# Last copies of the values in one tile of the input weights' buffers, attention's buffers allocated around it, and the expert gathers issued in order

## The chip, the cores and the metric

The kernel runs on one NeuronCore of one Trainium2 chip. The metric is the device time of one execution in microseconds (us). The kernel before was run three times; the median is what the change is compared with.

## What is computed

One block of a hybrid encoder in float32, with T = 1024 tokens and a width of 1024 (quoted with the parts that matter here; shapes in the comments are mine):

```python
proj = h @ w_in[l]                      # one projection for both mixers
aq, ak, av, iq, ik, iw, bq, bk, bv, br, bg = jnp.split(proj, split_points, axis=-1)
...                                     # rotary embedding of aq, ak, iq, ik
ya = dsa_mixer(aq, ak, av, iq, ik, iw)  # 8 heads of 64; each token sees the 256 best keys
...                                     # log_a from bg
ob = gla_mixer(bq, bk, bv, log_a)       # 4 heads, chunked linear attention
...
mix = jnp.concatenate([ya, yb], axis=-1) @ w_out[l]
h = layer_norm(DEEPNORM_ALPHA * h + mix, ln1_g[l], ln1_b[l])
ffn = hier_moe(h, ...)                  # router picks 2 of 32 experts per token
h = layer_norm(DEEPNORM_ALPHA * h + ffn, ln2_g[l], ln2_b[l])
```

An expert is `silu(x @ Wg) * (x @ Wu)` followed by a second product; its results are scaled by the gate and summed per token.

## The kernel before, in words

Float32 products are made as three products of split operands: each operand is cast to a high part (`whi`, `ehi`, `m`, `xh` ...) on ScalarE and the low part (`wlo`, `elo`, `xl` ...) is the difference, made on VectorE or GpSimd. The stages follow one another:

- **Input projections, index scores, top-k and the linear attention**, in an order chosen by a scheduler. The last product is `values(1, ...)` (L680): the attention values of the second half of the heads, four tiles of results in PSUM, each copied by ScalarE to a tile `vs` and stored by GpSimd's queue to the buffer `d_av` in HBM (L687, L688). The input weights live in a pool `wpool` whose raw, high and low weights have tags (`wraw`, `whi`, ...) with two or three buffers each.
- **Attention** (`attention`, L820 on), in an order written out by hand (`manual_schedule`): 32 items, four head pairs `hp` by eight query tiles `t`. For each item PE makes scores (`s`, L839), VectorE adds the selection bias and takes the maximum (`Sm`, `mx`, L844), ScalarE takes the exponential (L852), PE turns the weights (`pt`, L863), ScalarE or VectorE copies them out of PSUM to a tile `PT` (L866, L868), and PE multiplies them with the values into `ot` (L877). After every fourth query tile GpSimd spreads the reciprocals of the sums into `rb` (L910), PE turns them (L885), and the result goes to a tile `R` (L887, L888) and to the buffer `d_mix`. Attention's pool is allocated over the memory that `wpool` and the rest of the first stage give up, so its first writes into a place wait for the last readers of what lay there.
- **Output product, LayerNorm and router** (`out_phase`, L1007 to L1159), eight token tiles. For each tile the normalized row `r` is stored to `d_h` (which the experts gather from); then `r` is multiplied by ALPHA and stored to `d_y` (to which the experts' results are added). For tiles 0 to 6 that is `rows_out`; for tile 7 it is written out at the end (L1151, L1155, L1156). Meanwhile three pieces of the first expert's weights are split (`split_early`).
- **The change to the experts**: the route of the last tile gives `tok`, the list of tokens of each expert (`tok`, L1263). GpSimd gathers the rows of expert 0 and of expert 1 from `d_h` into `xg0` and `xg1` with indirect DMAs (L1427); `xg1` is set to zero first (L1319). Between them GpSimd makes `rvg` (L1267), from which the gates of the last tile come.
- **The expert stream** (`expert_stream`): 32 experts, each with four pieces of first-layer weights and two of second-layer weights, streamed by SyncE's queue. `ahead()` splits the next piece; `rows_in` issues the gather and turns the rows (L1420). A loop for experts with over 128 tokens and the last LayerNorm follow.

DMA queues keep the order of their engine: SP (SyncE) carries the weights and most loads, ACT carries the stores of `rows_out`, POOL (GpSimd) the gathers and the stores of the values.

Of the kernel before, what the change touches and what calls it, by code (L numbers as in the profile page):

```python
# [9 lines left out]
F32 = mybir.dt.float32  # L10
# [4 lines left out]
U32 = mybir.dt.uint32  # L15
AF = mybir.ActivationFunctionType
OP = mybir.AluOpType
# [3 lines left out]
T = 1024  # L21
# [143 lines left out]
class Kern:  # L165
# [514 lines left out]
    def values(self, g, w, tiles, queue=None):  # L680
        nc = self.nc
        queue = queue or nc.sync
        for t in tiles:

            vs = self.wpool.tile([128, 2, 2, 128], F32, name="vs", tag="wraw" if g and t > 2 else "vs", bufs=3 if g and t > 2 else 2)
            ps = yield from self.proj_n_steps(w, t)
            nc.scalar.copy(vs, ps.rearrange("p t (a b) -> p a t b", a=2))  # L687
            queue.dma_start(self.d_av[g][:, :, t:t + 2, :].rearrange("a p t c -> p a t c"), vs)  # L688
# [131 lines left out]
    def attention(self, p, before):  # L820
# [60 lines left out]
        def shares(s):  # L881

            rp = self.bank("pt", [128, 4, 128])
            for i in range(4):
                nc.tensor.transpose(rp[:, i, :], s["rb"][:, 2 * i:2 * i + 2, :].rearrange("p a b -> p (a b)"), ident)  # L885
            R = p.tile([128, 4, 128], F32, name="R", bufs=2)
            nc.scalar.copy(R.rearrange("p a b -> p (a b)"), rp.rearrange("p a b -> p (a b)"))  # L887
            nc.vector.tensor_mul(R, R, s["ot"])  # L888
            nc.sync.dma_start(self.d_mix[s["t"] // 4][:, :, s["hp"], :].rearrange("t p q -> p t q"), R)

        rec = ot = done = None
        with self.tc.manual_schedule(engines={mybir.EngineType.PE, mybir.EngineType.Activation, mybir.EngineType.DVE}):
            for n in range(len(items) + 2):
                new, turn = n if n < len(items) else None, n - 1 if 0 < n <= len(items) else None
                if new is not None:
                    hp, t = items[n]
                    loads = before(n)
                    if t % 4 == 0:
                        rec = p.tile([128, 4, 2], F32, name="rec", bufs=2)
                    st[n] = {"hp": hp, "t": t, "W": 128 * (t + 1), "S": [], "PT": [], "rec": rec, "loads": loads}  # L900
                if turn is not None:
                    s = st[turn]
                    if s["t"] % 4 == 0:
                        ot = self.bank("ot", [128, 4, 128])
                    s["ot"] = ot
                    if s["t"] % 4 == 3:
                        rb = s["rb"] = p.tile([128, 8, 64], F32, name="rb", bufs=2)
                        rr = p.tile([128, 8], F32, name="rr", bufs=2)
                        nc.vector.reciprocal(rr, s["rec"].rearrange("p a b -> p (a b)"))
                        nc.gpsimd.tensor_copy(rb, rr.unsqueeze(2).to_broadcast([128, 8, 64]))  # L910
                for hd in range(2):
                    if new is not None:
                        scores(new, hd)
                    if turn is not None:
                        turned(turn, hd)
                    if new is not None:
                        weights(new, hd)
                over, done = done, mixed(n - 2) if n > 1 else None
                if over:
                    shares(over)  # L920
            shares(done)
# [85 lines left out]
    def out_phase(self, ctx, weights):  # L1007
# [10 lines left out]
        with self.pool("outp") as p, self.pool("outm") as pm:  # L1018
# [52 lines left out]
                for j in range(4 * n, 4 * n + 4):  # L1071
                    nc.tensor.matmul(lg[:, :36], rT[:, j, :], wr[:, j, :], start=j == 0, stop=j == 7)  # L1072

            def rows_out(t, h):
                nc.scalar.dma_start(self.d_h[t * 128:(t + 1) * 128], h)

                nc.scalar.activation(h, h, AF.Copy, scale=ALPHA)
                nc.scalar.dma_start(self.d_y[t * 128:(t + 1) * 128], h)

            common = wsum, rb, g8, ones, before, lp  # L1080
            pending = None
            for t in range(NT - 1):
                mh, ml, x = operands(t)
                r = p.tile([128, D], F32, name="r", bufs=2)
                rT = p.tile([128, 8, 128], F32, name="rT")
                m, rs, half = self.moments(p, r)
                for n in range(2):
                    ps = self.bank("acc", [128, 512])
                    product(ps, n, range(8), mh, ml)
                    residual(r, x, ps, n)  # L1090
                    half(n)
                for n in range(2):
                    turned(r, rT, n)
                if t < NT - 2:
                    self.centre(r, m, gain)
                    self.scale(r, rs, shift)
                    with tc.issue_after(self.last_act.ins):
                        rows_out(t, r)

                if pending:  # L1100
                    for _ in self.route(p, *pending, *common):
                        pass
                lg = self.bank("ot", [128, 128])
                if t < NT - 2:
                    for n in range(2):
                        logits(lg, rT, n)
                pending = t, lg, m, rs

            mh, ml, x = operands(t + 1)
            r6, rT6, rs6, m6, lg6 = r, rT, rs, m, lg  # L1110
            r = p.tile([128, D], F32, name="r", bufs=2)
# [5 lines left out]
            with tc.manual_schedule(engines={mybir.EngineType.PE, mybir.EngineType.Activation, mybir.EngineType.DVE}):  # L1117
# [6 lines left out]
                steps = self.route(p, *pending, *common)  # L1124
                next(steps)
                self.scale(r6, rs6, shift)
                rows_out(t, r6)
                residual(r, x, ps[0], 0)
                half(0)
                turned(r, rT, 0)  # L1130
                product(ps[1], 1, range(4, 8), mh, ml)
                for _ in steps:
                    pass
# [14 lines left out]
                steps = self.route(p, t + 1, lg, m, rs, *common)  # L1148
                next(steps)
                self.scale(r, rs, shift)  # L1150
                nc.sync.dma_start(self.d_h[(t + 1) * 128:(t + 2) * 128], r)  # L1151
                for _ in steps:
                    pass
                early[1][0]()
                nc.scalar.activation(r, r, AF.Copy, scale=ALPHA)  # L1155
                nc.scalar.dma_start(self.d_y[(t + 1) * 128:(t + 2) * 128], r)  # L1156
                for e in early:
                    e[1]()
            self.lp = lp  # L1159

    def split_early(self):
# [29 lines left out]
    def route(self, p, t, lg, m, rs, wsum, rb, g8, ones, before, lp):  # L1191
# [69 lines left out]
        if end:  # L1261

            nc.vector.tensor_scalar(self.tok, lp[:, :, 0], float(PAD), None, op0=OP.add)  # L1263
            gates()
            rvg = [keep.tile([128, NE], F32, name=f"rvg{k}") for k in range(2)]
            for k in range(2):
                nc.gpsimd.tensor_scalar(rvg[k], self.oh[:, t, k, :], val[:, k, 1:2], None, op0=OP.mult)  # L1267

            def finish():
                for k in range(2):  # L1270
                    nc.tensor.matmul(lp[:, :, 1], sls[k], rvg[k], start=False, stop=k == 1, skip_group_check=True)
                nc.vector.tensor_copy(self.lists, lp)

            self.finish_gates = finish

    def count_blocks(self):
        nc, ones = self.nc, self.ones
# [18 lines left out]
    def experts(self):  # L1296
# [5 lines left out]
        with self.pool("exp") as self.ep:  # L1302
# [11 lines left out]
            with tc.manual_schedule(engines={mybir.EngineType.PE, mybir.EngineType.Activation, mybir.EngineType.DVE}):  # L1314
                third = self.split_early()
                third[0]()
                x = self.rows_in(self.xg[0], cols(0)[0])
                with tc.issue_after(self.last_gather.ins):
                    nc.gpsimd.memset(self.xg[1], 0.0)  # L1319
                third[1]()  # L1320
                self.expert_stream(cols, x, work)
            self.last_mm = None
# [14 lines left out]
    def expert_stream(self, cols, x, work):  # L1337
# [30 lines left out]
        for e in range(NE):  # L1368
            hg, hu = (self.bank("acc", [128, 512]) for _ in range(2))
            for q in range(4):  # L1370
# [5 lines left out]
                if q == 1:  # L1376
                    if e:

                        ah = self.turn_act(act)
                    else:  # L1380

                        x1 = self.rows_in(self.xg[1], cols(1)[0], ("y", "y"), 2)
                if e == 0 and q == 3:

                    self.ready.append(self.split_piece(self.piece()))
                    self.early.close()
                    self.wp = work.enter_context(self.pool("work"))
                elif q < 3:
                    ahead()
            act = self.gate_up(hg, hu)  # L1390
            if e:
# [29 lines left out]
                                                       src[:, 128 * (b + i):128 * (b + i) + 128], self.c["ident"])  # L1421
            self.split(hi[:, b:b + 4, :].rearrange("p a b -> p (a b)"), lo[:, b:b + 4, :].rearrange("p a b -> p (a b)"), pt)

    def rows_in(self, xg, tok, tags=("xh", "xl"), bufs=1):

        nc, p = self.nc, self.ep
        self.last_gather = nc.gpsimd.indirect_dma_start(out=xg, out_offset=None, in_=self.d_h,  # L1427
                                     in_offset=bass.IndirectOffsetOnAxis(ap=tok.bitcast(U32), axis=0),
                                     bounds_check=T - 1, oob_is_err=False)
        xh, xl = (p.tile([128, 8, 128], F32R, name=n, tag=t, bufs=bufs) for n, t in zip(("xh", "xl"), tags))  # L1430
        self.turn(xg, 8, xh, xl)
        return xh, xl
# [52 lines left out]
    def more_blocks(self):  # L1485
# [11 lines left out]
        we = self.I["we"].rearrange("e k c -> (e k) c")  # L1497
        wf = self.I["wf"].rearrange("e k c -> (e k) c")
        n = nc.values_load(self.nmore[0:1, 0:1], min_val=0, max_val=2 * T // 128)
        self.last_mm = None  # L1500
        with tc.For_i(0, n, 1):
            eh = p.tile([128, NE], F32, name="eh")
            e2 = p.tile([128, NE], F32, name="e2")
# [127 lines left out]
```

## Time and profile before

| what | value |
|---|---|
| median of 3 runs | 1294.08 us (1291.38 to 1295.2) |
| the profiled execution's own time | 1292.31 us |
| its span in the trace | 1290.5 us |
| mean granted TensorE clock | 0.97 |
| PE, DVE, ACT, POOL busy | 93%, 80%, 61%, 31% of the span |
| weights of the experts, 690 to 1200 us | 364 GB/s, PE 510.00 us busy |

The span is the time from the first to the last instruction of the trace; the execution's own time is 1.81 us longer. The rows quoted further down come from this one execution, and their start times are microseconds from the start of the span. A name in square brackets at a row's end says how long the engine had been idle and what released it.

### The profile page before, as it was taken

The numbers are of one execution on the slowest core, as the hardware profiler recorded it, in microseconds if no ns is written. First come the engines' busy times: TensorE is split into PE (matmuls) and PEld (weight loads), VectorE is DVE, ScalarE is ACT, GpSimd is POOL, SyncE is SP. The second block draws the span as 40 slices with busy tenths as digits, with TensorE's granted clock in tenths as the row PEclk, the third lists the DMA queues.
The fourth block names the chain that finished last, engine by engine and source line by source line (L and its number), as shares of the span: only waits on it lengthen the run. The fifth ranks groups of instructions, "written<-read, shape, count | busy, mean of one in ns | idle before, by whom it ended". The sixth has DMA issues, their size and how long they took to land.

```text
span 1290.5 us, 19395 instructions
## 1 busy us (share of the span) xinstructions
PE 1204.2 (93%) x6926; PEld 1003.1 (78%) x6926; DVE 1028.6 (80%) x1657; ACT 792.8 (61%) x1112; POOL 394.5 (31%) x354
## 2 busy tenths in 40 slices
PE   6999999999996999999859999999999999999962
PEld 5979988877795888888747888888888888888851
DVE  4567897999993666477768999889998899889945
ACT  4378366665534667132257777777777777777835
POOL 2532642345753453011121321112221222122215
PEclk9999999999998999999979999999999999999985
DMA  7653544325468661874378999999999999999926
GB/s 257 163 180 99 191 156 126 112 61 143 105 186 242 190 170 58 308 278 164 131 271 313 375 372 367 382 368 360 380 365 369 351 361 357 352 356 353 321 44 260
DMA packets 133588, 322.61 MB, mean 250 GB/s; under 512 B 20953, under 2 KB 50546, under 8 KB 133490
## 3 DMA queue, kind: packets, MB, share of 16 engines
q1 hardware_dynamic: 109826, 280.92, 61.4%
q0 software_dynamic: 15168, 26.27, 8.1%
q10 hardware_dynamic: 8496, 14.16, 3.3%
q8 instruction: 55, 0.90, 0.3%
q14 instruction: 43, 0.35, 0.1%
HBM read 283.78 MB, written 54.26 MB: 262 GB/s over the span
## 4 chain that ended last, share of the span: by engine, by line
PE 73%; DVE 8%; DMA 6%; ACT 5%; another core or an unknown queue 3%; POOL 3%; issue 3%; SPq 0%; ACTq 0%; POOLq 0%; DVEq 0%
PE acc L1353 26%; PE ot L1353 13%; PE acc L1057 7%; PE acc L236 5%; PE acc L222 4%; PE pt L1420 3%; PE ot L877 3%; DVE eq L723 3%; PE s L839 2%; PE pt L863 2%; PE g L236 1%; DMA d_mix<-ym 1%; PE ot L1072 1%; PE g L222 1%
## 5 line engine op out<-in xcount | busy, mean ns | idle before, releaser
L181 DVE TENSOR_TENSOR elo<-big,ehi 128x2048 fp32r<-128x2048 f32 (+1 forms) x132 | 268.0, 2062 | 21.9 <-ACT ehi L180 20.2
L180 ACT CAST ehi<-big 128x2048 fp32r<-128x2048 f32 (+1 forms) x132 | 223.0, 1727 | 0.0
L1353 PE MATMUL acc<-ehi,xh 128*128 128x512 f32 x512 | 206.4, 403 | 2.0 <-ACT sg L1469 2.0
L1353 PE MATMUL acc<-ehi,xl 128*128 128x512 f32 x512 | 203.3, 397 | 0.0
L1353 PE MATMUL acc<-elo,xh 128*128 128x512 f32 x512 | 203.2, 397 | 0.0
L1427 POOL DMA_INDIRECT xg<-d_h,tok x32 | 36.8, 1151 | 360.8 <-PE pt L1420 360.3
L222 PE MATMUL acc<-big,whi 128*128 128x512 f32 (+1 forms) x384 | 120.3, 392 | 10.0 <-ACT big L180 10.0
L1406 POOL DMA_INDIRECT d_y<-y,tok x32 | 96.2, 3006 | 105.8 <-ACT ehi L180 50.2
L236 PE MATMUL acc<-whi,big 128*128 128x256 f32 x672 | 125.4, 286 | 0.0
L1353 PEld LDWEIGHTS acc<-ehi,xh 128*128 128x128 f32 x512 | 96.7, 189 | 24.5 <-ACT sg L1469 2.4
L1353 PEld LDWEIGHTS acc<-ehi,xl 128*128 128x128 f32 x512 | 96.6, 189 | 23.6 <-DVE xl L181 0.3
L1353 PEld LDWEIGHTS acc<-elo,xh 128*128 128x128 f32 x512 | 97.0, 189 | 22.0
L236 PEld LDWEIGHTS acc<-whi,big 128*128 128x128 f32 x672 | 105.6, 192 | 1.8 <-issue 1.0
L723 DVE TENSOR_SCALAR_CACHE_REDUCE eq<-sc,cand 128x384 bf16<-128x384 f32 (+1 forms) x124 | 100.5, 810 | 7.0 <-POOL sc L735 4.6
L1353 PE MATMUL ot<-ehi,ah 128*128 128x512 f32 x256 | 104.1, 407 | 0.4 <-ACT ah L180 0.4
L181 DVE TENSOR_TENSOR elo<-slot,ehi 128x2048 fp32r<-128x2048 f32 (+1 forms) x46 | 95.5, 2102 | 7.8 <-ACT ehi L180 7.3
L1353 PE MATMUL ot<-ehi,al 128*128 128x512 f32 x256 | 101.5, 397 | 0.0
L1353 PE MATMUL ot<-elo,ah 128*128 128x512 f32 x256 | 101.4, 396 | 0.0
L753 ACT ACTIVATE sn<-sc,cand 128x896 bf16<-128x896 f32 (+1 forms) x62 | 68.0, 1097 | 46.5 <-DVE cand L749 36.5
L236 PE MATMUL acc<-wlo,big 128*128 128x256 f32 x336 | 95.8, 285 | 0.0
L222 PEld LDWEIGHTS acc<-big,whi 128*128 128x128 f32 x384 | 72.5, 193 | 25.1 <-ACT big L180 10.0
L1057 PE MATMUL acc<-wohi,m 128*128 128x512 f32 x256 | 86.0, 405 | 0.0
(297 smaller groups left out, 2601.6 us busy)
## 6 DMA issues: line engine op xcount, KB each, us to landing
big<-we SPq DMA_DIRECT2D x79, 1024.0 KB, 15.8
big<-wf SPq DMA_DIRECT2D x40, 1024.0 KB, 20.2
slot<-we SPq DMA_DIRECT2D x26, 1024.0 KB, 14.0
sc<-we SPq DMA_DIRECT2D x20, 1024.0 KB, 20.2
slot<-wf SPq DMA_DIRECT2D x16, 1024.0 KB, 23.2
wraw<-wi SPq DMA_DIRECT2D x52, 256.0 KB, 3.2
sc<-wf SPq DMA_DIRECT2D x8, 1024.0 KB, 10.5
raw<-xT SPq DMA_DIRECT2D x8, 512.0 KB, 6.9
```

The source lines that it names most:

```text
L180: nc.scalar.copy(hi, src)
L181: (lo_eng or nc.vector).tensor_tensor(lo, src, hi.bitcast(F32), op=OP.subtract)
L222: nc.tensor.matmul(ps[:m, :n], l[:, j, c0:c0 + m], r[:, j % 2, t0:t0 + n], start=(j == 0 and a == 0), stop=(j == 7 and a == 2))
L236: nc.tensor.matmul(ps[:, i, :], l[:, j % 2, s], r[:, j, :], start=(j == 0 and a == 0), stop=(j == 7 and a == 2))
L723: nc.vector.tensor_scalar(gtt[:, :WS[i]], x, v, 0.0, op0=op, op1=OP.add, accum_out=cnt[:, i:i + 1])
L753: nc.scalar.activation(jnk[:, :WS[i]], y[i], AF.Sign, bias=c, accum_out=cnt[:, i:i + 1])
L877: nc.tensor.matmul(ot[r, t % 4, :], v[:, b, r], s["PT"][hd][:, b, :], start=b == 0, stop=b == t)
L1057: nc.tensor.matmul(ps, l[:, j, :], w[:, j, s], start=(j == 0 and a == 0), stop=(j == 7 and a == 2))
L1353: nc.tensor.matmul(o, x[:, jj, :], w[:, j, s], start=(jj == 0 and a == 0), stop=(jj == n - 1 and a == 2))
L1406: nc.gpsimd.indirect_dma_start(out=self.d_y, out_offset=bass.IndirectOffsetOnAxis(ap=tok.bitcast(U32), axis=0), in_=y, in_offset=None, bou ...
L1420: self.last_mm = nc.tensor.transpose(pt[:, 128 * i:128 * i + 128], src[:, 128 * (b + i):128 * (b + i) + 128], self.c["ident"])
L1427: self.last_gather = nc.gpsimd.indirect_dma_start(out=xg, out_offset=None, in_=self.d_h, in_offset=bass.IndirectOffsetOnAxis(ap=tok.bitcas ...
```

## The change

The copies of the last product go into slices of one tile `whole` that uses a buffer of the tag `whi`, where the tiles `vs` were. In attention, the two buffers of `rb` and the two of `R` are allocated ahead of all others (with equal shapes), so that these lie over `whole` and the others elsewhere. `rows_out` writes the scaled rows to another tile than `r` (tile 6's to its `x`, tile 7's to `rT`), tile 6's call moves behind a turn, tile 7's ahead of the rest of the route, and the two early low parts are made in the other order. At the change to the experts GpSimd issues the memset and the gathers of expert 0 and 1 before `rvg`, and in the first expert one `ahead()` moves ahead of the turning of expert 1's rows.

```diff
@@ values
+        whole = self.wpool.tile([128, 4, 2, 2, 128], F32, name="whole", tag="whi", bufs=2) if g else None
         for t in tiles:
-
-            vs = self.wpool.tile([128, 2, 2, 128], F32, name="vs", tag="wraw" if g and t > 2 else "vs", bufs=3 if g and t > 2 else 2)
+            vs = whole[:, t // 2] if g else self.wpool.tile([128, 2, 2, 128], F32, name="vs", bufs=2)
@@ attention
+        for name in ("rb", "R"):
+            for _ in range(2):
+                p.tile([128, 512], F32, name=name, bufs=2)
         with self.tc.manual_schedule(engines={mybir.EngineType.PE, mybir.EngineType.Activation, mybir.EngineType.DVE}):
@@ out_phase
-            def rows_out(t, h):
-                nc.scalar.dma_start(self.d_h[t * 128:(t + 1) * 128], h)
-
-                nc.scalar.activation(h, h, AF.Copy, scale=ALPHA)
-                nc.scalar.dma_start(self.d_y[t * 128:(t + 1) * 128], h)
+            def rows_out(t, h, x, queue):
+                queue.dma_start(self.d_h[t * 128:(t + 1) * 128], h)
+
+                nc.scalar.activation(x, h, AF.Copy, scale=ALPHA)
+                nc.scalar.dma_start(self.d_y[t * 128:(t + 1) * 128], x)
...
-                rows_out(t, r6)
                 residual(r, x, ps[0], 0)
                 half(0)
                 turned(r, rT, 0)
+                rows_out(t, r6, x6, nc.scalar)
...
-                nc.sync.dma_start(self.d_h[(t + 1) * 128:(t + 2) * 128], r)
+                rows_out(t + 1, r, rT.rearrange("p a b -> p (a b)"), nc.sync)
                 for _ in steps:
                     pass
                 early[1][0]()
-                nc.scalar.activation(r, r, AF.Copy, scale=ALPHA)
-                nc.scalar.dma_start(self.d_y[(t + 1) * 128:(t + 2) * 128], r)
-                for e in early:
+                for e in reversed(early):
                     e[1]()
+                self.ready.reverse()
@@ experts
-                x = self.rows_in(self.xg[0], cols(0)[0])
+                self.last_gather = nc.gpsimd.memset(self.xg[1], 0.0)
+                for e in range(2):
+                    self.gather(self.xg[e], cols(e)[0])
                 with tc.issue_after(self.last_gather.ins):
-                    nc.gpsimd.memset(self.xg[1], 0.0)
+                    self.start_gates()
+                x = self.turn_rows(self.xg[0])
@@ expert_stream
-                        x1 = self.rows_in(self.xg[1], cols(1)[0], ("y", "y"), 2)
+                        ahead()
+                        x1 = self.turn_rows(self.xg[1], ("y", "y"), 2)
...
-                elif q < 3:
+                elif q < 3 and (e or q != 1):
                     ahead()
```

`start_gates()` makes the two `rvg`; `gather` is the indirect DMA of `rows_in`, `turn_rows` is its rest.

GpSimd at the change to the experts stood like this before (`rvt` and `rvg` are the routed tables of the last tile, `xg_7168` is expert 0's and every second later expert's gathered rows, `xg_7279` expert 1's):

```order
L1227 TENSOR_SCALAR rvt<-oh,K 128x32 x2
L1267 TENSOR_SCALAR rvg_7250<-oh,val 128x32
L1267 TENSOR_SCALAR rvg_7251<-oh,val 128x32
L1427 DMA xg_7168<-d_h,tok 128x1024
L1319 MEMSET xg_7279 128x1024
L1427 DMA xg_7168<-d_h,tok 128x1024
L1427 DMA xg_7279<-d_h,tok 128x1024 x2
```

And it stands like this after (`xg_7169` is expert 0's, `xg_7278` expert 1's):

```order
L1232 TENSOR_SCALAR rvt<-oh,K 128x32 x2
L1324 MEMSET xg_7278 128x1024
L1443 DMA xg_7169<-d_h,tok 128x1024
L1443 DMA xg_7278<-d_h,tok 128x1024
L1274 TENSOR_SCALAR rvg_7253<-oh,val 128x32
L1274 TENSOR_SCALAR rvg_7254<-oh,val 128x32
L1443 DMA xg_7169<-d_h,tok 128x1024
L1443 DMA xg_7278<-d_h,tok 128x1024
```

The first gather no longer stands behind `rvg`, the memset is ahead of it, and expert 1's gather follows directly, where expert 2's (the second one into expert 0's buffer) stood between.

ScalarE from the end of the router to the first activation of expert 0 (the last `f` is in the route of tile 7; `ehi` are high parts of expert weights, `xh` those of gathered rows, `sg` the activated half of the first product) stood like this before:

```order
L1222 ACTIVATE f<-f 128x1
L1170 CAST ehi<-raw 128x512 x4
L1170 CAST ehi<-big 128x512 x4
L1155 ACTIVATE r<-r 128x1024
L1156 DMA d_y<-r 128x1024
L180 CAST xh<-pt 128x512 x2
L180 CAST ehi<-big 128x1024 x2
L180 CAST xh<-pt 128x512 x2
L180 CAST ehi<-extra 128x1024 x2
L180 CAST ehi<-big 128x1024 x4
L1469 ACT_TABLE_LOAD
L1469 ACTIVATE sg<-acc 128x512
```

And it stands like this after:

```order
L1227 ACTIVATE f<-f 128x1
L1082 ACTIVATE rT<-r 128x1024
L1083 DMA d_y<-rT 128x1024
L1175 CAST ehi<-raw 128x512 x4
L1175 CAST ehi<-big 128x512 x4
L180 CAST xh<-pt 128x512 x2
L180 CAST ehi<-big 128x1024 x2
L180 CAST ehi<-extra 128x1024 x2
L180 CAST xh<-pt 128x512 x2
L180 CAST ehi<-big 128x1024 x4
L1488 ACT_TABLE_LOAD
L1488 ACTIVATE sg<-acc 128x512
```

The scaling of tile 7's rows and its store moved ahead of two times four casts, and the cast of the piece `extra` ahead of the casts of expert 1's rows.

## Rows read from the trace of the kernel before

**Rows 1.** The page's head, and its chain by engine

```profile
span 1290.5 us, 19395 instructions
...
PE 73%; DVE 8%; DMA 6%; ACT 5%; another core or an unknown queue 3%; POOL 3%; issue 3%; SPq 0%; ACTq 0%; POOLq 0%; DVEq 0%
```

**Rows 2.** Stretches: length, busy time by engine (instructions), PE clock, DMA share, GB/s

```profile
393.00:397.60 4.60, 3.15 (x20) 2.16 (x18) 1.80 (x15) 4.14 (x13) 4.60 (x7) 1.00 0.94 269
397.60:406.50 8.90, 0.08 (x1) 0.00 (x0) 0.39 (x2) 0.00 (x0) 0.68 (x1) 0.69 0.89 274
406.50:411.00 4.50, 4.45 (x16) 2.95 (x16) 2.36 (x8) 2.78 (x8) 0.00 (x0) 0.50 0.95 281
...
525.00:640.00 115.00, 115.00 (x626) 95.18 (x625) 76.60 (x274) 27.45 (x57) 13.83 (x29) 1.00 0.63 229
...
690.00:1200.00 510.00, 510.00 (x2368) 414.66 (x2366) 466.08 (x330) 384.05 (x313) 118.51 (x57) 1.00 1.00 364
```

**Rows 3.** The chain that ended last, at attention's start: start, length, what

```profile
396.10 9.93 DMA d_av<-vs
```

**Rows 4.** Timeline of PE in head pairs 0 and 1

```profile
406.55 0.66 PE L863 MATMUL pt<-K,Sm 128*128 128x128 f32 x2 [8.87 <-DVE PT L866]
407.14 0.70 PE L877 MATMUL ot<-PT,kq 128*64 128x128 f32 x4
...
413.98 0.88 PE L877 MATMUL ot<-PT,kq 128*64 128x128 f32 x12
...
423.03 0.66 PE L885 MATMUL pt<-K,rb 128*128 128x128 f32 x4
...
437.20 0.44 PE L877 MATMUL ot<-PT,big 128*64 128x128 f32 x4
437.57 0.66 PE L885 MATMUL pt<-K,rb 128*128 128x128 f32 x4
...
442.91 0.88 PE L877 MATMUL ot<-PT,big 128*64 128x128 f32 x12
```

**Rows 5.** Timeline of ACT, start of the output product

```profile
526.04 1.14 ACT L180 CAST m<-mraw 128x512 fp32r<-128x512 f32 x2 [2.38 <-DMA d_mix<-R]
537.71 1.22 ACT L180 CAST m<-mraw 128x512 fp32r<-128x512 f32 x2 [10.53 <-DMA mraw<-d_mix]
```

**Rows 6.** The chain that ended last, at the change to the experts

```profile
647.03 3.02 DMA d_h<-r
...
651.63 8.21 DMA xg<-d_h,tok
```

**Rows 7.** Timeline at the change to the experts

```profile
649.37 2.09 POOL L1267 TENSOR_SCALAR rvg<-oh,val 128x32 f32<-128x32 bf16 x2 [2.22 <-issue]
...
651.21 0.33 ACTq L1156 DMA_DIRECT2D d_y<-r  x1
...
652.98 0.97 POOL L1319 MEMSET xg<- 128x1024 f32 x1
...
659.97 1.94 PE L1420 MATMUL pt<-K,xg 128*128 128x128 f32 x8 [11.24 <-DMA xg<-d_h,tok]
```

**Rows 8.** DMA issues, 644 to 664 us: count, median us to landing

```profile
xg<-d_h,tok POOLq DMA_INDIRECT x3, 5.4
```

**Rows 9.** Timeline of ACT and PE in expert 0

```profile
669.71 1.08 ACT L180 CAST xh<-pt 128x512 fp32r<-128x512 f32 x2 [5.29 <-PE pt L1420]
670.67 2.01 ACT L180 CAST ehi<-extra 128x1024 fp32r<-128x1024 f32 x2
672.57 3.90 ACT L180 CAST ehi<-big 128x1024 fp32r<-128x1024 f32 x4
676.49 1.28 ACT L1469 ACT_TABLE_LOAD   x1
...
678.43 0.50 PE L1353 MATMUL acc<-ehi,xh 128*128 128x512 f32 x1 [2.00 <-ACT sg L1469]
```

**Rows 10.** Waits for DMA, 700 to 1200 us: total, times, longest

```profile
DVE elo L181 <- DMA sc<-we: 1.1, 1, 1.1
```

More of the change, by code (lines that the diff above doesn't have):

```diff
@@ L885, in shares @@
                 nc.tensor.transpose(rp[:, i, :], s["rb"][:, 2 * i:2 * i + 2, :].rearrange("p a b -> p (a b)"), ident)
-            R = p.tile([128, 4, 128], F32, name="R", bufs=2)
+            R = p.tile([128, 512], F32, name="R", bufs=2).rearrange("p (a b) -> p a b", b=128)
             nc.scalar.copy(R.rearrange("p a b -> p (a b)"), rp.rearrange("p a b -> p (a b)"))
@@ L906, in attention @@
                     if s["t"] % 4 == 3:
-                        rb = s["rb"] = p.tile([128, 8, 64], F32, name="rb", bufs=2)
+                        rb = s["rb"] = p.tile([128, 512], F32, name="rb", bufs=2).rearrange("p (a b) -> p a b", b=64)
                         rr = p.tile([128, 8], F32, name="rr", bufs=2)
@@ L1097, in out_phase @@
                     with tc.issue_after(self.last_act.ins):
-                        rows_out(t, r)
+                        rows_out(t, r, r, nc.scalar)
                 if pending:
@@ L1107, in out_phase @@
                 pending = t, lg, m, rs
+            x6 = x
             mh, ml, x = operands(t + 1)
@@ L1265, in route, with rows @@
             rvg = [keep.tile([128, NE], F32, name=f"rvg{k}") for k in range(2)]
-            for k in range(2):
-                nc.gpsimd.tensor_scalar(rvg[k], self.oh[:, t, k, :], val[:, k, 1:2], None, op0=OP.mult)
+            def rows():
+                for k in range(2):
+                    nc.gpsimd.tensor_scalar(rvg[k], self.oh[:, t, k, :], val[:, k, 1:2], None, op0=OP.mult)
             def finish():
@@ L1272, in finish @@
                 nc.vector.tensor_copy(self.lists, lp)
-            self.finish_gates = finish
+            self.start_gates, self.finish_gates = rows, finish
     def count_blocks(self):
@@ L1422, in turn, with rows_in, gather, turn_rows @@
             self.split(hi[:, b:b + 4, :].rearrange("p a b -> p (a b)"), lo[:, b:b + 4, :].rearrange("p a b -> p (a b)"), pt)
[L1424 to L1429, printed above, removed]
+    def rows_in(self, xg, tok):
+        self.gather(xg, tok)
+        return self.turn_rows(xg)
+    def gather(self, xg, tok):
+        with self.tc.issue_after(self.last_gather.ins) if self.last_gather else nullcontext():
+            self.last_gather = self.nc.gpsimd.indirect_dma_start(
+                out=xg, out_offset=None, in_=self.d_h, in_offset=bass.IndirectOffsetOnAxis(ap=tok.bitcast(U32), axis=0),
+                bounds_check=T - 1, oob_is_err=False)
+    def turn_rows(self, xg, tags=("xh", "xl"), bufs=1):
+        p = self.ep
         xh, xl = (p.tile([128, 8, 128], F32R, name=n, tag=t, bufs=bufs) for n, t in zip(("xh", "xl"), tags))
@@ L1499, in more_blocks @@
         n = nc.values_load(self.nmore[0:1, 0:1], min_val=0, max_val=2 * T // 128)
-        self.last_mm = None
+        self.last_mm = self.last_gather = None
         with tc.For_i(0, n, 1):
```

## The prediction, made before the changed kernel ran

> **What bounds the kernel now.** I began with the chain of the page: PE makes up 73% of it, VectorE 8% and DMA 6% [rows 1]. A PE-bound kernel gains where PE stands still, so I looked for the places at which the change touches such a stretch. Cutting the span into stretches shows where there is nothing to gain: PE is busy 115.00 of 115 us through the output product and the router, and 510.00 of 510 in the expert stream [rows 2]. Three holes remain that the edits touch.
>
> The first is the start of attention. PE is busy 0.08 of 8.90 us between 397.60 and 406.50 [rows 2], and the chain says why: 9.93 us are the landing of a store `d_av<-vs` [rows 3]. The row of PE behind it waited 8.87 us for VectorE's copy to `PT` [rows 4], and that copy could not be made sooner because the buffers of `PT` lie where the `vs` tiles of the last product lay, which the store still reads. That is a wait for memory, not for data: the product that made the values had ended before. The granted clock is 1.00 before the hole, 0.69 on average in it, and 0.50 (the 1.2 GHz level) in the 4.50 us behind it, in which PE is busy for 4.45 [rows 2]: the hole costs more than its own length.
>
> The second is the change to the experts. PE waits 11.24 us for the gathered rows of expert 0 [rows 7]; the chain is the landing of `d_h` (3.02 us from 647.03) and then the gather's flight, 8.21 us from 651.63 [rows 6]. The third is a stall of 2.00 us at 678.43, in which PE waits for the first activation of expert 0 [rows 9].
>
> **The change part by part.**
>
> *Attention's start.* The last copies go to `whole`, and only `rb` and `R` lie over it. By the addresses in the changed kernel, `PT`, `Sm` and the small tiles lie over weights and tables whose last readers were done before attention begins (the last of them PE itself). So the first copy to `PT` no longer waits for a store. The hole is worth 8.87 us [rows 4]. I take all of it: the operands were there at 397.6, since PE had turned two blocks before it stopped.
>
> To this comes the slow clock. From the product of four matmuls to that of twelve, head pair 0 takes 413.98 - 407.14 = 6.84 us and head pair 1, with the same items, 442.91 - 437.20 = 5.71 [rows 4]. That is 1.13 us, and head pair 1 has four more transposes in it (the row at 437.57, 0.66 us at most), so between 1.1 and 1.8; I take 1.5. The attention part is 8.87 + 1.5 = 10.4 us, with the bounds 8.9 (the clock falls anyway) and 10.7.
>
> *What waits for the store now.* `rb` does. GpSimd writes it for the first time for the shares that PE turns at 423.03 [rows 4], which will be 423.03 - 10.4 = 412.6. The store lands at 406.0 [rows 3], GpSimd's copy behind it is a single instruction, and behind that on GpSimd there is only the splitting of the output weights. So some 5 us of slack cover it; if they were gone, each us more would cost one. At the other end of attention, the tile `x` of token tile 1 lies over `R`, so its load on SP's queue waits for the last store of `R`, which released ScalarE at 526.04 in the kernel before [rows 5] (there `m` waited for it, which it no longer does). Behind that load on SP stand two weight pieces and the loads of tile 2's operands, which ScalarE took at 537.71 after an idle stretch of 10.53 us [rows 5]. I price this at nothing: eight tiles in 115 us are 14.4 us each, so tile 2 is needed near 525 + 2 x 14.4 = 553.8, and the load is late by one or two us.
>
> *The gather of expert 0.* Before, GpSimd made `rvg` in 2.09 us from 649.37 and gathered then [rows 7]. After, `rvg` is behind the gathers and the memset (0.97 us [rows 7]) takes the place of GpSimd's idle 2.22 us. The gather waits for the landing of `d_h` at 647.03 + 3.02 = 650.05 [rows 6], and with some 0.6 us of issue starts near 650.7 in place of 651.63: 0.9 us. Its flight is the uncertain part. The 8.21 us were next to the store `d_y<-r`, issued at 651.21 [rows 7]. That store is now issued behind the scaling of the row, which no longer stands behind eight casts and can start when `d_h` is issued at 647.03 [rows 6]: some 3 us earlier, so that it is mostly gone by then. The median of the three gathers there is 5.4 us [rows 8]. I take the middle of 5.4 and 8.21, 6.8 us, since the weight loads still run and expert 1's gather now follows directly. Landing near 657.5 in place of 659.84: 2.3 us. The bounds are 0 (a flight of 9.1) and 3.7 (5.4). ScalarE's two groups of casts start some 2 us later for it, which PE's wait of 11.24 us covers [rows 7].
>
> *The activation.* Before, ScalarE was idle 5.29 us until 669.71, and had then xh (1.08), `extra` (2.01) and the next pieces (3.90) to cast ahead of the table load (1.28) [rows 9]. Now `extra` is cast in the idle stretch, as its buffer is free once PE is done with the first of the four pieces, and PE is in the second one while ScalarE idles. The table load then ends 2.01 us earlier against PE, and of the 2.00 us of stall some 0.2 remain: the last cast must wait for a buffer that PE frees. Gain 1.8, bounds 0 and 2.0. The other moves (tile 6's scaled rows, the order of the early low parts, a swap of memset and cast on VectorE) I cost at nothing: PE does not wait in that stretch at all, and the low parts are made while PE waits for the gather; without that cover a swap would cost one cast, 1.0 us (two take 2.01 [rows 9]).
>
> *Does an earlier start survive the stream?* The stream moves 364 GB/s with a DMA share of 1.00, yet PE is busy throughout [rows 2], and in 500 us only 1.1 us of waiting for a load is seen on any engine [rows 10]. So PE paces it, and what is gained ahead of it stays. The Trainium skill's page "DMA: Bandwidth & Descriptors" (sections "Specifications" and "Where 436 GB/s comes from") gives about 358 GB/s as the limit of HBM for one core, and says that this side binds transfers from HBM to SBUF. By that rule the stream would run at its limit, the weights would set its end, and the sum would be 10.4 and not 14.5. The trace's 364 GB/s over 510 us is over that limit, and the engines do not wait; by the row the sum stays.
>
> **The sum.** 10.4 + 2.3 + 1.8 = 14.5 us. Against the profiled execution's own 1292.31 that is 1277.8. That execution is 1.77 below the median, which gives 1279.6 from there. I forecast 1278.5, between the two.
>
> **The rivals.**
>
> *The hand-over gives nothing (14%).* The gather's flight stays long since expert 1's rows and `extra` now fly beside it (9 of the 14), or the stream is paced by its loads and gives the earlier start back (5). For the latter speaks the DMA share of 1.00 in the stream [rows 2]; against it that nobody waits there [rows 10]. Then only attention's 10.4 stays: 1292.3 - 10.4 = 1281.9.
>
> *Another wait takes the place of the store's (13%).* `rb` is reached before its memory is free, or another store of the first stage (the turned keys) still reads memory that attention writes first. The DMA queues are 0.89 to 0.95 busy in that stretch [rows 2], so stores are slow to land. If half of the 10.4 comes back, 1283.0; if all of it, 1288.2. It decides from a landing later than 412.6, 6 us after the one in rows 3.
>
> *The change does not do what it says (3%).* Neither wait goes: 1292 to 1294.
>
> *Slower (3%).* `x` of tile 1 holds SP's queue behind the landing of `R`, and the operands of tile 2 and the weight pieces come late into a stretch in which PE has no idle time [rows 2]. With a slack of 553.8 - 537.7 = 16 us it costs from a hold of 16 us on, and the kernel gets slower than before only from 16 + 14.5 = 30 us on. In the kernel before, the store released its waiter after 2.38 us of idle [rows 5].
>
> **How the numbers follow.** The forecast itself has 67%. Its own range takes in the bounds of its terms: at best 10.7 + 3.7 + 2.0 = 16.4, which is 1275.9 from the profiled execution; at worst 8.9 + 0 + 0, which is 1283.4 from there and 1285.2 from the median. With runs that differ by some 2 us to either side of the profiled one, 1274 to 1285. The first rival is inside that, and the second ends at 1288.2; so 1273 to 1288 leaves out the last two rivals and little more. A difference from no change can be told from about 0.3%, 3.9 us, so from 1290.2 down it is faster. All of the forecast, the first rival and most of the second are below that: faster 0.92, same 0.05, slower 0.03.
>
> **What the profile after would show.** Right: no wait of PE over 1 us near 397 to 407, no `d_av` landing in the chain there, the clock at 1.00 through it, the row with twelve matmuls near 403.6; the first gather starting near 640.3 (650.7 - 10.4) with a flight of 6 to 7 us; PE's wait for `sg` below 0.5 us; the stream's length unchanged. Wrong: a wait of GpSimd for `rb` that PE's turning of the shares then shows, a flight of the gather over 8 us, a wait of VectorE or ScalarE for weights in the stream, or a wait for `mraw` that PE feels at tile 2.

## The result, and the profile after

The changed kernel takes 1278.80 us in the median of 4 runs (1275.02 to 1284.24), the kernel before 1294.01 beside it; the ratio is 0.9893, with a 95% interval of 0.9872 to 0.9914. The forecast was 1278.5. The execution that was profiled is the slowest of the four, 1284.24, so I also show rows of a second profiled execution of the same kernel (e4 below, 1274.97, the fastest of its six) where they differ. The page's head and its chain by engine, as [rows 1]:

```profile
span 1282.4 us, 19393 instructions
...
PE 74%; DVE 8%; DMA 6%; ACT 4%; another core or an unknown queue 3%; issue 2%; POOL 1%; ACTq 0%; SPq 0%; POOLq 0%; DVEq 0%
```

The stretches that answer to [rows 2]:

```profile
393.00:397.60 4.60, 2.98 (x25) 2.78 (x24) 0.92 (x3) 1.24 (x2) 3.46 (x4) 1.00 0.70 176
397.60:406.50 8.90, 7.23 (x32) 5.45 (x32) 4.01 (x22) 6.52 (x20) 5.13 (x7) 0.62 0.97 270
406.50:411.00 4.50, 4.50 (x42) 3.94 (x42) 3.42 (x9) 3.74 (x9) 0.00 (x0) 1.00 0.70 223
...
680.00:1190.00 510.00, 510.00 (x2366) 414.57 (x2365) 466.02 (x331) 383.81 (x314) 117.32 (x57) 1.00 0.99 362
```

PE is busy 7.23 us where it was busy 0.08, though in this execution at a granted clock of 0.62; the stream is what it was. Attention's start on PE's timeline, as [rows 4], and ScalarE's next to it:

```profile
395.59 0.39 PE L840 MATMUL s<-kq,kq 128*128 128x256 f32 x2
398.32 0.90 PE L840 MATMUL s<-kq,kq 128*128 128x256 f32 x4 [2.34 <-ACT whole L688]
...
403.35 0.70 PE L878 MATMUL ot<-PT,kq 128*64 128x128 f32 x4
...
409.32 0.88 PE L878 MATMUL ot<-PT,kq 128*64 128x128 f32 x12
...
396.46 0.62 ACT L180 CAST so_hi<-rp 128x512 fp32r<-128x512 f32 x1 [2.47 <-DMA d_k<-so_hi]
397.68 2.05 ACT L688 COPY whole<-acc 128x512 f32<-128x512 f32 x4 [0.60 <-ACT so_hi L180]
```

The same place in the kernel before began like this:

```profile
393.24 0.39 PE L839 MATMUL s<-kq,kq 128*128 128x256 f32 x2
393.85 0.74 PE L839 MATMUL s<-kq,kq 128*128 128x256 f32 x4 [0.22 <-ACT vs L687]
395.71 0.33 PE L863 MATMUL pt<-K,Sm 128*128 128x128 f32 x1 [1.11 <-ACT Sm L852]
```

The store's landing is no longer in front of PE. But the first stage ended 2.35 us later than in the kernel before (the first score product is at 395.59, there at 393.24), and PE waits 2.34 us for the copies to `whole`. ScalarE keeps its order: the copies stand behind the cast of the last keys, `so_hi`, which waited for the landing of an earlier store of keys, and that came late. The same stretch in the second profiled execution:

```profile
391.92 0.63 PE L840 MATMUL s<-kq,kq 128*128 128x256 f32 x4
...
395.55 0.44 PE L878 MATMUL ot<-PT,kq 128*64 128x128 f32 x4
...
400.52 0.88 PE L878 MATMUL ot<-PT,kq 128*64 128x128 f32 x12
409.60 0.66 PE L886 MATMUL pt<-K,rb 128*128 128x128 f32 x4
...
388.33 0.62 ACT L180 CAST so_hi<-rp 128x512 fp32r<-128x512 f32 x1 [0.99 <-DMA d_k<-so_hi]
405.76 0.61 POOL L915 COPY rb<-rr 128x512 f32<-128x512 f32 x1 [10.83 <-DMA d_av<-whole]
```

Here the keys' cast was done 3 us before the last product ended, and PE has no wait over 0.16 us; the granted clock is 1.00 from 391.92 to 406.50. `rb` now waits for the store and is made 3.2 us before PE turns it. The change to the experts in the first execution, the chain and the timeline, as [rows 6, 7, 9]:

```profile
642.35 3.02 DMA d_h<-r
...
646.32 7.62 DMA xg<-d_h,tok
```

```profile
643.52 0.33 ACTq L1083 DMA_DIRECT2D d_y<-rT  x1
...
654.08 1.94 PE L1431 MATMUL pt<-K,xg 128*128 128x128 f32 x8 [9.46 <-DMA xg<-d_h,tok]
...
670.93 0.50 PE L1363 MATMUL acc<-ehi,xh 128*128 128x512 f32 x1 [0.53 <-ACT sg L1488]
```

The stall of 2.00 us is down to 0.53 (1.47 less). From the issue of `d_h` to PE's turn it was 659.97 - 647.03 = 12.94 us, and is 654.08 - 642.35 = 11.73.

### The profile page after: what moved, and what is told of

Same layout as the page of the kernel before. It is cut to its first block, busy times and chain, and to the rows that moved or that the text cites. A ratio compares the mean times of both kernels' runs of the same rounds, so it can differ in the third digit from the quotient of the medians.

```text
span 1282.4 us, 19393 instructions
## 1 busy us (share of the span) xinstructions
PE 1206.6 (94%) x6926; PEld 1006.3 (78%) x6926; DVE 1026.6 (80%) x1657; ACT 792.0 (62%) x1112; POOL 388.7 (30%) x354
## 4 chain that ended last, share of the span: by engine, by line
PE 74%; DVE 8%; DMA 6%; ACT 4%; another core or an unknown queue 3%; issue 2%; POOL 1%; ACTq 0%; SPq 0%; POOLq 0%; DVEq 0%
PE acc L1363 26%; PE ot L1363 13%; PE acc L1062 7%; PE acc L236 5%; PE acc L222 4%; PE pt L1431 3%; DVE eq L724 3%; PE ot L878 3%; PE s L840 3%; PE pt L864 2%; DMA d_mix<-ym 2%; PE g L222 2%; PE g L236 1%; PE acc L482 1%
## 5 line engine op out<-in xcount | busy, mean ns | idle before, releaser
L1417 POOL DMA_INDIRECT d_y<-y,tok x32 | 91.5, 2858 | 109.5 <-ACT ehi L180 66.5
```

The lines of the kernel that those rows point to most:

```text
L1417: nc.gpsimd.indirect_dma_start(out=self.d_y, out_offset=bass.IndirectOffsetOnAxis(ap=tok.bitcast(U32), axis=0), in_=y, in_offset=None, bou ...
```

## The experiments

Two measures recur, both read from PE's timeline, and both leave out how late the stage in question began: **attention's start**, from the first score product to the product of twelve matmuls (20.74 us in the kernel before, 413.98 - 393.24), and **the gather**, in two parts: from the issue of `d_h` to the start of expert 0's gather, and on to PE's turn of its rows.

**e1, the edits of `values` and `attention` alone**

```diff
+        whole = self.wpool.tile([128, 4, 2, 2, 128], F32, name="whole", tag="whi", bufs=2) if g else None
...
+        for name in ("rb", "R"):
...
             # out_phase, route, experts and expert_stream as before
```

> The edits of values and attention alone; everything behind attention as before. My theory: the wait for the store of the values and the slow clock behind it are gone, worth 10.4 us, near 1283.6. Rival (in the profiled execution of the changed kernel PE still stood 2.3 us for the last copies, which ScalarE had queued behind a cast of the keys): the hole is replaced in part, worth 7 us, near 1287. If the gain were all at the change to the experts: 1294.

1279.42 us beside 1291.14 of the kernel before, ratio 0.9910 (0.9882 to 0.9937): 11.7 us, more than the 10.4 of the theory and the 7 of the rival. Attention's start takes 8.61 us, 12.1 less than before:

```profile
391.56 0.63 PE L840 MATMUL s<-kq,kq 128*128 128x256 f32 x4
...
400.17 0.88 PE L878 MATMUL ot<-PT,kq 128*64 128x128 f32 x12
```

**e2, the edits at the change to the experts alone**

```diff
             # values and attention as before
+                rows_out(t + 1, r, rT.rearrange("p a b -> p (a b)"), nc.sync)
...
+                for e in range(2):
+                    self.gather(self.xg[e], cols(e)[0])
```

> The edits of out_phase, route, experts and expert_stream alone; values and attention as before. My theory: 4.1 us (2.3 of the gather, 1.8 of the activation), near 1289.9, and the store's wait of about 9 us at attention's start stays. By the profiled execution of the changed kernel: 2.8 us (1.2 and 1.6), near 1291.2. Rival that the stream of weights gives the earlier start back: 1294, with waits for DMA in the stream.

1290.04 us, ratio 0.9981 (0.9964 to 0.9998): 1.1 us, and the interval reaches from 0.3 to 4.6. The two traces are sharper: 11.68 us from `d_h` to PE's turn (12.94 before) and 0.53 us of stall (2.00). The store's wait at attention's start is 9.3 us there, and in e1 the gather (12.82 us) and the stall (1.99) are much as in the kernel before, so each half acts at its own place. The medians of the halves add up to 12.8 us, where the whole gains 14.5 on the same chip (e4, 1276.67); the intervals are wider than that difference.

**e3, the last copies on VectorE**

```diff
-            nc.scalar.copy(vs, ps.rearrange("p t (a b) -> p a t b", a=2))
+            (nc.vector.tensor_copy if g else nc.scalar.copy)(vs, ps.rearrange("p t (a b) -> p a t b", a=2))
```

> The changed kernel with the four last copies of the values made by VectorE, behind its last top-k row, in place of ScalarE, where they stand behind the cast of the last keys. If that queue is the wait that took the place of the store's: 2 to 3 us below the changed kernel, and PE's wait for the copies is below 0.5 us. If it was one disturbed execution: no difference from the changed kernel.

**e4, the changed kernel once more**

> The changed kernel once more, for a second profiled execution. If the 2.3 us by which its last input product ended later than before is scatter between executions: it ends elsewhere between 391 and 396 now, and the time is within 3 us of 1278.8. If the change itself delays the first stage: it ends near 395.6 again. PE's wait for ScalarE's copies: near 2.3 us again if the queue behind the keys is the rule, below 0.5 if it was chance.

e3 takes 1277.21 us and e4, on the same chip, 1276.67: the queue behind the keys is no regular price. In e4's trace the first stage ended at 391.92 and attention's start took 8.60 us. In e3's it took 9.97, because the scores' exponentials still stand behind the same cast on ScalarE. The wait of 2.34 us in the first profiled execution is one that comes in some executions: PE waits 2.12 us for the copies to `whole` in e8, and in e10 2.50 us at the same product, where the row names a load of keys but ScalarE's copies, behind the same cast, begin only at 393.68.

**e5, e6, e9: what sets the gather's landing.** e5 puts `rvg` between the two gathers, e6 puts the scaling and the store of tile 7 back behind the casts, e9 puts `rvg` ahead of the gathers and the memset behind the first, as before, with the early store kept.

```diff
 e6
-                rows_out(t + 1, r, rT.rearrange("p a b -> p (a b)"), nc.sync)
+                nc.sync.dma_start(self.d_h[(t + 1) * 128:(t + 2) * 128], r)
...
                 early[1][0]()
+                x = rT.rearrange("p a b -> p (a b)")
+                nc.scalar.activation(x, r, AF.Copy, scale=ALPHA)
+                nc.scalar.dma_start(self.d_y[(t + 1) * 128:(t + 2) * 128], x)
 e9
+                self.start_gates()
+                self.last_gather = None
+                self.gather(self.xg[0], cols(0)[0])
+                with tc.issue_after(self.last_gather.ins):
+                    self.last_gather = nc.gpsimd.memset(self.xg[1], 0.0)
+                self.gather(self.xg[1], cols(1)[0])
```

> The changed kernel with the gather of expert 1 behind rvg, and so 1.4 us later, not right behind that of expert 0. In four executions with the changed order it takes 7.65 to 7.76 us from the first gather's start to PE's turn of its rows, where I had expected some 6.8. If expert 1's rows slow expert 0's: 6.8 to 7.2 here. If the weight loads set the flight: 7.65 again.

> The changed kernel with the scaling of the last tile's rows and their store to d_y at the old place, behind eight casts. If the store beside the gather is what made the flight 8.2 to 8.3 us in the kernel before: 8.2 again here, 0.6 us more than in the changed kernel. If it does not matter: 7.65.

> The changed kernel with GpSimd's order at the change to the experts as before (rvg ahead of the gathers, the memset behind the first); the early store stays. In the changed kernel it takes 11.7 us from the issue of d_h to PE's turn of expert 0's rows, in the kernel before 12.9, with the late store alone 13.1. If the earlier start of the gather has a share of its own: 12.3 here. If the store's place is all of the gain: 11.7.

These three and e7 ran once each (1277.27, 1276.69, 1276.45 and 1278.71 us for e5, e6, e9 and e7), so they are read from their traces and not from their times. e5's timeline at that place:

```profile
639.68 1.27 POOL L1443 DMA_INDIRECT xg<-d_h,tok  x1 [3.00 <-DVE elo L1179]
643.85 1.09 POOL L1443 DMA_INDIRECT xg<-d_h,tok  x1 [0.16 <-POOL rvg L1274]
647.38 1.94 PE L1431 MATMUL pt<-K,xg 128*128 128x128 f32 x8 [9.45 <-DMA xg<-d_h,tok]
```

e6's:

```profile
632.79 0.35 SPq L1157 DMA_DIRECT2D d_h<-r  x1
636.80 0.33 ACTq L1163 DMA_DIRECT2D d_y<-rT  x1
636.83 1.24 POOL L1446 DMA_INDIRECT xg<-d_h,tok  x1 [3.03 <-DVE elo L1182]
645.88 1.94 PE L1434 MATMUL pt<-K,xg 128*128 128x128 f32 x8 [10.83 <-DMA xg<-d_h,tok]
```

And e9's:

```profile
634.63 0.36 SPq L1080 DMA_DIRECT2D d_h<-r  x1
635.80 0.33 ACTq L1083 DMA_DIRECT2D d_y<-rT  x1
639.22 1.35 POOL L1444 DMA_INDIRECT xg<-d_h,tok  x1 [0.17 <-issue]
646.92 1.94 PE L1432 MATMUL pt<-K,xg 128*128 128x128 f32 x8 [10.61 <-DMA xg<-d_h,tok]
```

| kernel | `d_h` to the gather | gather to PE's turn | sum |
|---|---|---|---|
| before | 4.60 | 8.34 | 12.94 |
| e1, everything behind attention as before | 4.59 | 8.23 | 12.82 |
| changed (first execution, e4) | 3.97, 4.05 | 7.76, 7.65 | 11.73, 11.70 |
| e5, second gather later | 4.01 | 7.70 | 11.71 |
| e6, late store | 4.04 | 9.05 | 13.09 |
| e9, old order on GpSimd | 4.59 | 7.70 | 12.29 |

The second gather does not slow the first: e5 issues it 4.17 us behind the first in place of 1.53 in e4 (2.6 us later, more than the 1.4 I had expected), and the flight is 7.70. The Trainium skill's page "DMA: Bandwidth & Descriptors", section "Queues, rings and completion order", says of DMAs issued by SyncE and ScalarE that on each SDMA engine descriptors are consumed in ring order; these two gathers come from GpSimd, and the 7.70 us fit the same order there. The store next to the gather does slow it, by more than I had expected: 9.05 against 7.64 to 7.81 in the nine traces that have the early store and the weight loads as they are. With the late store the earlier start buys nothing (13.09 against 12.94 and 12.82); with the early store it is worth 12.29 - 11.71 = 0.6 us, and the store alone is worth 0.5 to 0.65 (12.29 against 12.82 and 12.94).

**e7, the cast of `extra` back behind expert 1's rows**

```diff
-                        ahead()
                         x1 = self.turn_rows(self.xg[1], ("y", "y"), 2)
-                elif q < 3 and (e or q != 1):
+                elif q < 3:
```

> The changed kernel with the cast of the piece extra behind the casts of expert 1's rows again, as before. If the order of these casts is the whole of the stall: PE waits 2.0 us for the first activation again, 0.5 in the changed kernel. If the earlier gather of expert 1 did it: 0.5 here too.

The stall is back, on PE's timeline:

```profile
665.26 0.50 PE L1363 MATMUL acc<-ehi,xh 128*128 128x512 f32 x1 [1.99 <-ACT sg L1487]
```

The order of these casts is the whole of it.

**e8, `whole` without the early allocation**

```diff
-        for name in ("rb", "R"):
-            for _ in range(2):
-                p.tile([128, 512], F32, name=name, bufs=2)
```

> The changed kernel without the early allocation of rb and R: the tile whole stays, but by the addresses a score tile Sm and the sums rec lie over it now. My theory: the wait for the store of the values comes back at attention's start, this time on VectorE's scores, and PE stands for 8 to 11 us. Rival: moving the copies to the other buffer is enough and the early allocation only tidies: no wait of PE over 1 us there.

1295.59 us in its one run, beside 1300.06 in the one run of the kernel before on that chip. Its waits around attention's start (engine, what it waited for, total, times, longest):

```profile
DVE Sm L845 <- DMA d_av<-whole: 18.9, 1, 18.9
PE s L840 <- DVE mx L845: 13.6, 1, 13.6
```

The wait is back and longer: attention's start takes 26.19 us. Of the 4.7 us by which PE waits longer than in the kernel before, 1.4 come from the score tile being needed earlier than `PT` (PE stops 3.02 us after its first score product, 4.44 in the kernel before). Some 3.2 come from the store, which lands 15.97 us after that product in place of 12.80; in this execution the copies were late, behind the cast of the keys. Moving the copies gains nothing by itself; what lies over them decides.

**e10 and e11, the weight loads held back.** Both hold the next slot loads until GpSimd has issued both gathers, by a memset of one column of the first slot; e11 also loads `extra` ahead of the slots and does not hold it (its trace has that load at 639.89 us, between the two gathers, and the slots' from 641.50 on).

```diff
-            for _ in range(2):
-                self.next_raw()
...
-            for _ in range(2):
-                self.next_raw()
...
                 with tc.issue_after(self.last_gather.ins):
+                    nc.gpsimd.memset(self.slots[-3][:, 0, 0:1], 0.0)
                     self.start_gates()
+                    self.last_load = None
+                    k = self.pieces                                                    # e11 alone
+                    ORDER[k:k + 4] = sorted(ORDER[k:k + 4], key=lambda n: n != 4)      # e11 alone
+                    for _ in range(4):
+                        self.next_raw()
```

> The changed kernel with the next four loads of weights (4 MB) held back until GpSimd has issued both gathers, by a memset of one column of the first slot. If these loads set the gather's flight: 4 to 6 us from its start to PE's turn in place of 7.65, and the kernel is 2 to 3 us faster than the changed one unless the piece extra then comes late. If the flight is the gather's own: 7.65, and no gain.

> The changed kernel with the slots' loads held back as in e10, but the piece extra loaded ahead of them and not held back. If e10 lost only by the lateness of extra: PE turns expert 0's rows some 9 to 10 us after the issue of d_h (11.7 in the changed kernel), the wait for the first activation is 0.5 us again, and the kernel is 1.5 to 2.5 us faster than the changed one. If the weights held back are missed later too: waits for DMA in the stream, and no gain.

> The changed kernel a third time, beside e11 on the same chip: 11.7 us from the issue of d_h to PE's turn, a wait of 0.5 us for the first activation, and a median within 3 us of 1278.

e10's timeline:

```profile
639.02 0.35 SPq L1080 DMA_DIRECT2D d_h<-r  x1
642.62 1.68 POOL L1443 DMA_INDIRECT xg<-d_h,tok  x1 [2.59 <-DVE val L1249]
647.50 1.94 PE L1431 MATMUL pt<-K,xg 128*128 128x128 f32 x8 [6.21 <-DMA xg<-d_h,tok]
...
659.61 2.00 ACT L180 CAST ehi<-extra 128x1024 fp32r<-128x1024 f32 x2 [7.66 <-DMA extra<-we]
668.32 0.79 PE L1363 MATMUL acc<-ehi,xh 128*128 128x512 f32 x1 [3.99 <-ACT sg L1488]
```

The flight is 4.88 us with the loads held back: they account for some 2.8 us of it. The gather also starts earlier, 3.60 us after `d_h` in place of 4.04 (e12), since `d_h` lands in 2.64 us and not in 3.09. But `extra`, held behind them, is now what ScalarE waits for (7.66 us), and the stall that follows is 3.99 us; the kernel takes 1282.95 beside 1291.17 of the kernel before. Not all of that is `extra`: from `d_h` to PE's turn of the third expert's rows it takes 42.56 us in place of 39.90 in e4, and the profiled execution lost 4.5 us more at attention's start (13.06 against 8.60). e11's timeline:

```profile
634.43 0.36 SPq L1080 DMA_DIRECT2D d_h<-r  x1
638.03 1.69 POOL L1445 DMA_INDIRECT xg<-d_h,tok  x1 [2.59 <-DVE val L1249]
643.25 1.94 PE L1433 MATMUL pt<-K,xg 128*128 128x128 f32 x8 [6.55 <-DMA xg<-d_h,tok]
...
660.09 0.50 PE L1365 MATMUL acc<-ehi,xh 128*128 128x512 f32 x1 [0.53 <-ACT sg L1490]
```

8.82 us from `d_h` to PE's turn and 0.53 us of stall: 1274.78 us in the median, ratio 0.9872 (0.9845 to 0.9898), beside 1277.57 of the changed kernel (e12), whose attention's start took 8.60 us again. The median is 2.8 us lower, as the trace says (11.78 - 8.82 = 2.96); the two intervals of the ratios overlap.

## Why the prediction was right

**The sum held, its parts less so.** I had 10.4 us for attention, 2.3 for the gather and 1.8 for the activation, 14.5 together; the first medians differ by 15.2. From the traces, attention's start gained 12.1 us in most executions of the changed kernel, the gather 1.2 and the activation 1.5: 14.8. The waits that I named were the ones that went, but one term was too small by 1.7 us and the two others too large by 1.4 together; that the sum came out so close is luck.

**The store's wait (8.87 us) and the slow clock (1.5 us).** Right in kind: e1 shows that these edits alone bring the gain, and e8 that it hangs on what lies over `whole`. From the first score product to the product of four matmuls it took 407.14 - 393.24 = 13.90 us, and takes 395.55 - 391.92 = 3.63 in e4: 10.3 us, not 8.9. PE had also waited 0.22 and 1.11 us there for ScalarE, which in that execution was behind the keys; I had left that out. From four to twelve matmuls it took 6.84 us and takes 400.52 - 395.55 = 4.97: 1.9 us for the clock. My bounds ended at 10.7, so the truth was outside this term's bounds.

**Another wait in its place (13%).** It appeared in some executions, but from a place that I had not named: not `rb` (made in time) but the copies to `whole` themselves, behind the cast of the last keys on ScalarE. The store of the turned keys was in this rival only as a reader of memory that attention writes; here it held that cast up. So two of my signs failed in the first profiled execution: PE waited 2.34 us at 398.32, and the granted clock was 0.62 from 397.60 to 406.50. In the first profiled execution attention's start took 409.32 - 395.59 = 13.73 us, and 13.06 in e10's, against 8.60 to 8.85 in seven of the other executions that have both edits of attention (e5 and e3: 9.24 and 9.97). It comes and goes with the moment at which the store of the keys lands: the cast waited 2.47 us for it there and 0.99 in e4. What moves that moment stays open. That the 2.35 us by which the first stage ended late are scatter follows from e4 (391.92, before the old kernel's 393.24).

**The gather (2.3 us).** This is the term that I mis-sized: 1.2 us. I took the middle between 5.4 us and 8.21 for the flight, on the thought that the store would be out of the way. It is, and is worth 0.5 to 0.65 us, but 2.4 to 2.9 us of the flight that is left come from the weight loads, as e10 and e11 show with 4.88 and 5.22 us. The earlier start is 0.6 us in place of 0.9: GpSimd needs 0.95 us from the landing of `d_h` at 645.37 to the gather at 646.32, where I had put 0.6.

**The activation (1.8 us).** 1.5, by the cast of `extra` alone (e7). Of the stall 0.49 to 0.53 us stay in the traces with the new order, e10 apart, and not 0.2.

**The stream gives nothing back.** PE's turns of gathered rows at the two ends of the stream, in the kernel before and then in the changed one:

```profile
689.52 1.03 PE L1420 MATMUL pt<-K,xg 128*128 128x128 f32 x8
1198.66 1.03 PE L1420 MATMUL pt<-K,xg 128*128 128x128 f32 x8
...
682.01 1.04 PE L1431 MATMUL pt<-K,xg 128*128 128x128 f32 x8
1191.15 1.03 PE L1431 MATMUL pt<-K,xg 128*128 128x128 f32 x8
```

It is 7.51 us earlier at both. The limit of 358 GB/s of the Trainium skill's page "DMA: Bandwidth & Descriptors" (section "Specifications") would have taken the hand-over's gain back; the trace moves 362 GB/s with PE busy throughout, and disagrees. The load of `x` behind `R`'s store, the way in which it could have become slower, cost nothing: tile 2's cast is at 532.84 in place of 537.71, 4.87 us earlier, where the whole stretch is 4.68 earlier at its end (the issue of `d_h`).

## What to carry to other kernels

When a stage starts by writing into memory that the last stage's stores still read, look at what lies there: put the buffer that is needed last over it, and the wait is covered, while the same store under a buffer that is needed first cost 17.6 us at that place in e8 (26.19 against 8.60), more than the whole gain, though part of it was that execution's late store. A transfer that PE waits for is priced by what the queues carry next to it, so look at what is issued just before it and is not needed soon; holding that back was worth more here than starting the transfer earlier (e11 against e9), provided that the one load that is needed soon goes first (e10). And a term read from one execution includes that execution's own accidents: measure it over a stretch whose both ends are in the stage.

## What the runs showed of the hardware that I had not expected

The granted clock fell to 0.50 in a stretch in which PE stood nowhere. Its last wait ahead of that stretch, 0.3 us, is there as well in e4, where the clock stayed at 1.00. In e2 the output product begins behind 32 small matmuls of 36 columns (L1026); these stretches show it:

```profile
520.00:525.00 5.00, 5.00 (x47) 4.83 (x43) 2.08 (x4) 1.62 (x3) 0.00 (x0) 0.89 0.35 86
525.00:530.00 5.00, 5.00 (x13) 3.94 (x14) 1.76 (x4) 1.14 (x2) 0.00 (x0) 0.50 0.99 391
530.00:535.00 5.00, 5.00 (x22) 3.98 (x21) 1.05 (x2) 0.00 (x0) 0.00 (x0) 0.93 1.02 413
```

PE is busy 5.00 of 5.00 us at 1.2 GHz. From the first of the 32 small matmuls to the first turn of `r` (L1067 in e2) it takes 18.16 us in e2 and 16.59 to 16.61 in e1, e3 and e10, against 15.06 in the kernel before and 15.05 in e4, with the same matmuls in the same order: the slow clock cost 3.1 us in e2 and 1.5 in the other three. What decides whether the clock falls there stays open. The end of the first stage moved too, between 2.2 us before that of the kernel before and 2.4 us behind it. Between the three profiled executions of the changed kernel the clock did not fall at this place, and the end of the first stage and attention's start make up 8.80 of the 9.2 us between the spans of the first and e4, and 1.57 of the 2.4 us between e12 and e4. Whether it is why e1's and e2's medians say less than their traces is not shown, as only one execution of each left a trace.
